# Down-projections of the prompt as seven block products, and small VectorE operations with one SBUF operand

## The chip, the core and the metric

The kernel runs on one core of a Trainium2 chip. Its engines work side by side, each through its own queue: TensorE (PE) multiplies matrices into the eight banks of PSUM, VectorE (DVE), ScalarE (ACT) and GpSimd (POOL) work on rows, and SyncE (SP) issues the transfers. The metric is the device time of one execution in microseconds. The time of a kernel is the median of its runs.

## What is computed

The reference is a two-layer streaming encoder for 1024 prompt tokens and 8 x 16 sample tokens, 1152 rows of 1024 features in float32. Layer 0 has windowed attention with sinks, layer 1 chunk-band attention on keys and values that are projected once from the output of layer 0. In each layer the attention is followed by a gated MLP with a causal convolution. Both parts end in a layer norm over the residual:

```python
u = h @ w_up                      # 1024 -> 2 x 2816
y = conv_b                        # width 3, along the tokens
for tap in range(CONV_W):
    y = y + conv_w[tap] * ue[:, tap:tap + T]
a, g = jnp.split(y, 2, axis=-1)
out = (jax.nn.gelu(g) * a) @ w_down   # 2816 -> 1024: the down-projection
...
x = layer_norm(DEEPNORM_ALPHA * x + (1 + g_f) * f, ln_g[l, 1], ln_b[l, 1])
```

## The kernel before

**Operands in two parts.** Every matmul operand is kept as a rounded part (hi) and the rest (lo), and a product is three matmuls: lo x hi, hi x lo and hi x hi. `split` (L176) makes them: a cast on ScalarE (L167) writes hi, and a subtraction (L178) with two SBUF inputs writes lo, on VectorE or on GpSimd as the caller says.

**Order.** The program is written out in order, and a scheduler places the instructions of each engine from that order, from the buffers that are free, and from a model of the time. `Ring` (L55) hands out buffers in turn, so a buffer that is still in use makes the next writer wait. SyncE issues all the transfers through one queue.

**Up-projection** (`ffn`, L1218). The 2816 hidden features are 22 blocks of 128. Blocks 0 and 1 are made by plain products (`plain`). The other 20 (`spair`) make one value block and one gate block together by seven block products instead of eight (`products`, L1131; the matmul is L1203): the token rows of H are split in halves of 64 tokens within each tile, the weights in halves of their inputs, and sums of blocks stand on both sides. For each row block GpSimd makes four weight sums of 128x512 (L1151 to L1154), ScalarE and VectorE split seven half weights into the ring `sub` of eight half slots, and the PSUM results are added up by VectorE (L1164) or copied by ScalarE (L1162, L1171). Then follow the convolution (L1289 on ScalarE, L1250 on VectorE, L1259 on GpSimd for the sample rows), the gelu (L1296), the product with the value half on GpSimd (L1297), and the store of the gated block of 1152 tokens to `actD` in DRAM (L1298). In layer 0 the modulation vectors of later parts (`ada`) are multiplied in the background of this stage.

**Down-projection** (`down`, L1350). The nine token tiles (8 prompt tiles, and the sample tile 8) are taken in three groups of three. For each group all 22 weight blocks are loaded again (128x1024, 512 KB) with their activations (128x384, 192 KB). `fetch` splits the weights through ScalarE and GpSimd, the activations through ScalarE and VectorE (L1379). `mm` (L1386) runs three matmuls of 512 columns for each tile and each output half. At the end of a group `evict` multiplies the six banks by the gate (L1399, VectorE), and `tail` reads the residual (L1405 in layer 0, L1411 and L1414 in layer 1) and norms the row. In the last group the last 4 or 6 weight blocks (`KEEP`) are kept back and done tile by tile, so that a tile can be finished while the next one is multiplied.

**Tails.** In layer 0 `norm_tail` (L1002) takes the statistics (`stats`, L971 with L975 to L979, and `rsqrt`, L962), norms the row on VectorE (L1006), transposes it on PE (L1016), applies the next modulation by L1028 (ScalarE) or L1024 (VectorE, the chunks in `VA`) and `sample_affine` (L1050, L1051), copies the transposed row (L1032), splits it into H (GpSimd), scales it (L1039, L1040), and stores three rows of 512 KB. In layer 1 `norm_last` (L983) ends the row either by two VectorE operations (L993, L994; tiles in `VT`) or by ScalarE, GpSimd and VectorE in turn (L997, L998, L999).

**After layer 0** `kv` (L824) projects V for nine tiles in two halves, and K by seven products. Its block sums on the token side (`tsums`, L1100) need the normed rows of all tiles.

**Small operations.** In the attention of layer 0 the sink is added to the row sums (L613 for four elements, L699 for one), and `rsqrt` ends with a product of two single columns (L969). All of these have two SBUF inputs.

## Time and profile before

| | us |
|---|---|
| median of 3 runs | 2810.72 (2810.69 to 2818.3) |
| the profiled execution | 2808.31 |
| its span, first to last instruction | 2806.5 |
| down stage of layer 0 / layer 1, from the start of its first to the start of its last matmul | 285.2 / 276.0 |

In the rows of the profile, `PE` is TensorE, `PEld` its weight loads, `DVE` VectorE, `ACT` ScalarE, `POOL` GpSimd and `SP` SyncE. A group of instructions is written as line, engine, operation, output<-inputs by tile name, form and count, then busy us, the mean ns of one, and the idle time of its engine in front of it with what ended that. Where a row has three numbers with slashes, they are the shortest, the median and the longest duration in ns. The names are those of the program: F and ws hold float32 data, wh, wl and X weights, H the input rows, xa (X1) the sums of rows or the activations, C small vectors.

### The profile page before, as it was taken

How to read it: one execution, taken by the hardware profiler on the slowest of the kernel's cores; microseconds unless marked ns; L12 is line 12 of the kernel's file. 1: busy time of each engine (PE TensorE's matmuls, PEld its weight loads, DVE VectorE, ACT ScalarE, POOL GpSimd, SP SyncE). 2: the span in 40 equal slices, each digit the busy share in tenths (PEclk: the TensorE clock that was granted, in tenths of full speed). 3: DMA queues.
4: the chain of work that ended last, by engine and by line, in shares of the span. 5: the costliest groups of instructions: out<-in, count | busy, mean ns of one | idle time of the engine just before them, and what ended most of it. 6: DMA issues, size and time to landing. Idle time of an engine off the chain costs nothing.

```text
span 2806.5 us, 46569 instructions
## 1 busy us (share of the span) xinstructions
PE 2701.0 (96%) x17398; PEld 2384.3 (85%) x17398; DVE 1898.8 (68%) x3622; ACT 1307.8 (47%) x2607; POOL 1117.7 (40%) x755
## 2 busy tenths in 40 slices
PE   7999889999999999999999999989999999999997
PEld 5897768989999998777898888867899999998886
DVE  4376768776666684766854667766887777774764
ACT  3375633533333343443536666663444444444442
POOL 2132523444333457565220121242444333458662
PEclk9999999999999999999999999999999999999999
DMA  7656434474444446665757457763432222247662
GB/s 291 212 157 198 146 98 173 146 250 142 143 156 145 142 132 220 214 225 195 266 199 268 120 153 192 221 202 122 170 123 71 72 80 71 71 143 256 210 199 76
DMA packets 205187, 467.96 MB, mean 167 GB/s; under 512 B 34752, under 2 KB 97936, under 8 KB 204960
## 3 DMA queue, kind: packets, MB, share of 16 engines
q1 hardware_dynamic: 204960, 464.98, 51.0%
q8 instruction: 137, 2.24, 0.3%
q14 instruction: 90, 0.74, 0.1%
HBM read 365.17 MB, written 109.17 MB: 169 GB/s over the span
## 4 chain that ended last, share of the span: by engine, by line
PE 40%; DVE 4%; DMA 3%; ACT 2%; issue 1%; POOL 0%; SPq 0%; POOLq 0%; DVEq 0%; ACTq 0%
PE PS L1203 18%; PE PS L1386 10%; PE PS L296 4%; PE PS L309 4%; PE PS L590 1%; PE PS L568 1%; PE PS L540 1%; DVE F L507 1%; DMA F<-hmD 1%; PE PS L543 1%; ACT F L919 1%; PE PS L717 0%; DVE wl L178 0%; DMA F<-hD 0%; DVE xa L178 0%
## 5 line engine op out<-in xcount | busy, mean ns | idle before, releaser
L1203 PE MATMUL PS<-H,wh 128*128 128x320 f32 (+1 forms) x2752 | 427.9, 298 | 0.0
L1203 PEld LDWEIGHTS PS<-H,wh 128*128 128x128 f32 x2752 | 390.3, 192 | 0.4 <-issue 0.4
L1164 DVE TENSOR_TENSOR F<-PS,F 128x256 f32<-128x256 f32 (+1 forms) x446 | 197.7, 453 | 199.7 <-PE PS L1203 198.9
L167 ACT CAST wh<-F 128x512 fp32r<-128x512 f32 (+3 forms) x265 | 168.0, 645 | 328.3 <-PE PS L1203 186.6
L1379 DVE TENSOR_TENSOR xa<-xa 128x384 fp32r<-128x384 f32 x132 | 180.8, 1379 | 190.5 <-ACT xa L167 189.0
L1250 DVE SCALAR_TENSOR_TENSOR F<-F 128x1024 f32<-128x1024 f32 x320 | 258.9, 855 | 4.5 <-ACT F L1289 3.4
L178 DVE TENSOR_TENSOR wl<-F,wh 128x512 fp32r<-128x512 f32 (+2 forms) x236 | 215.0, 924 | 61.9 <-ACT wh L167 61.5
L1203 PE MATMUL PS<-H,wl 128*128 128x320 f32 (+1 forms) x1376 | 244.0, 300 | 8.7 <-ACT F L1171 7.2
L296 PE MATMUL PS<-H,wh 128*128 128x384 f32 (+1 forms) x1152 | 225.1, 339 | 0.0
L1386 PE MATMUL PS<-wh,xa 128*128 128x512 f32 x696 | 222.0, 395 | 0.0
L178 POOL TENSOR_TENSOR wl<-ws,wh 128x1024 fp32r<-128x1024 f32 x59 | 148.6, 2523 | 178.8 <-ACT wh L167 144.1
L1203 PEld LDWEIGHTS PS<-H,wl 128*128 128x128 f32 x1376 | 205.1, 192 | 16.9 <-ACT F L1171 7.7
L1203 PE MATMUL PS<-xa,wh 128*128 128x320 f32 (+1 forms) x1408 | 216.6, 296 | 1.4 <-DVE xa L178 1.4
L167 ACT CAST wh<-ws 128x512 fp32r<-128x512 f32 (+1 forms) x159 | 126.8, 804 | 190.8 <-PE PS L1203 94.8
L296 PEld LDWEIGHTS PS<-H,wh 128*128 128x128 f32 x1152 | 200.9, 189 | 1.3 <-issue 0.8
L1203 PEld LDWEIGHTS PS<-xa,wh 128*128 128x128 f32 x1408 | 197.4, 189 | 2.1 <-DVE xa L178 1.7
L1259 POOL TENSOR_TENSOR F<-F 128x16 f32<-128x16 f32 x88 | 47.8, 543 | 312.4 <-DVE F L1250 220.5
L1386 PEld LDWEIGHTS PS<-wh,xa 128*128 128x128 f32 x696 | 130.6, 188 | 30.7
L167 ACT CAST xa<-xa 128x384 fp32r<-128x384 f32 x132 | 67.4, 513 | 187.6 <-DMA xa<-actD 181.9
L309 PE MATMUL PS<-wh,H 128*128 128x512 f32 (+1 forms) x576 | 145.7, 367 | 1.4 <-DVE F L1095 0.8
L628 POOL TENSOR_TENSOR F<-F,X 64x512 f32<-64x512 f32 x62 | 79.5, 1282 | 169.6 <-DVE F L604 147.7
L1297 POOL TENSOR_TENSOR F<-F 128x1152 f32<-128x1152 f32 x44 | 119.8, 2722 | 49.5 <-DVE F L1250 31.3
(269 smaller groups left out, 6193.0 us busy)
## 6 DMA issues: line engine op xcount, KB each, us to landing
ws<-in_wdn_dram SPq DMA_DIRECT2D x66, 512.0 KB
F<-in_wdn_dram SPq DMA_DIRECT2D x66, 512.0 KB
ws<-in_adaw_dram SPq DMA_DIRECT2D x64, 512.0 KB
actD<-F SPq DMA_DIRECT2D x44, 576.0 KB
xa<-actD SPq DMA_DIRECT2D x132, 192.0 KB
ws<-in_wup_dram SPq DMA_DIRECT2D x49, 512.0 KB
F<-in_adaw_dram SPq DMA_DIRECT2D x48, 512.0 KB
F<-in_wup_dram SPq DMA_DIRECT2D x39, 512.0 KB
```

Of the source, the lines that this page charges most:

```text
L167: nc.scalar.copy(out, in_)
L178: self.eng(el).tensor_sub(lo, src, hi.bitcast(F32))
L296: mm = self.nc.tensor.matmul(out[:, 0:n], w[a][:, k * 128 : k * 128 + 128], H[:, p, k, s0 : s0 + n], start=i == 0, stop=i == 23)
L309: self.nc.tensor.matmul(out[:, 0:n], H[:, p, j * kn + k, t0 : t0 + 128], w[a][:, k * n : k * n + n], start=i == 0, stop=i == 23,)
L628: self.eng("v" if last else "p").tensor_mul(on[r, q], on[r, q], rb[r, :])
L1164: nc.vector.tensor_add(d, v(ps), a if len(a.shape) == 3 else v(a))
L1203: self.pairmm = nc.tensor.matmul(ps[:, 0:m], w[a][:, k * 128 : k * 128 + 128], x(p, k, n), start=start and c == 0, stop=c == 11, skip_grou ...
L1250: nc.vector.scalar_tensor_tensor(o, u, cw[:, cc, i : i + 1], o, op0=ALU.mult, op1=ALU.add)
L1259: nc.gpsimd.tensor_add(y3[:, :, 0:2], y3[:, :, 0:2], E4[:, cc])
L1297: nc.gpsimd.tensor_mul(yg, yg, ya)
L1379: nc.vector.tensor_sub(lo, raw, hi.bitcast(F32))
L1386: self.downmm = nc.tensor.matmul(ps, a[p][:, i * 128 : i * 128 + 128], w[q][:, hf * 512 : hf * 512 + 512], start=j == 0 and c == 0, stop=j ...
```

## The change

**Seven products for the down-projection.** Two neighbouring weight blocks (an even one and an odd one) form a pair; there are 11 pairs. The prompt is split in two halves of four tiles, the output in two halves of 512 columns. Per pair, GpSimd makes four sums of the activations (`act_sums`) and four of the weights (`weight_sums`), during the up-projection, and both go to DRAM (`actS`, `wT`). Then come seven products one after the other, in the order 1, 2, 5, 6, 3, 7, 4, each over the 11 pairs with four tiles: one weight half and one activation half per step. The sample tile is no part of the seven: it rides as a fifth tile in products 1, 2, 5 and 6, with plain operands. The results are combined on ScalarE and VectorE between the products. Both splits of a step now have their subtraction on VectorE.

**What moves with it.** The gated rows get three fixed buffers (one for the value half, two for the gate half) in place of a ring of three, because the sums overwrite two of them in place. One of the four weight slots becomes the buffer of the weight sums, so `sub` has six half slots. The tails of tiles 8, 0, 1, 2 and 3 run inside products 3 and 7, those of 4 to 7 behind product 4. In layer 0 these last four alternate with the first five V tiles of `kv`. The norm of the tails of layer 0 goes from VectorE to ScalarE (`norm_rows`), all modulations to ScalarE (`VA` is empty), and the scaling product to GpSimd. The tiles X2 and the first weight slot are taken anew with another type between the stages.

**Small operations.** L969, L699 and L996 become operations with one SBUF input and a scalar column; L613 becomes a reduction over a pair of columns.

The core of the diff:

```diff
-GR = ((0, 1, 2), (6, 7, 8), (3, 4, 5))
-GB = ((6, 7, 0, 1, 2, 3), (4, 5, 6, 7, 0, 1), (2, 3, 4, 5, 6, 7))
-TBG = ((2, 3), (0, 1), (0, 1))
+NK = NFF // 2
 NPL = 2
 KEEP = (4, 6)
+TAILS = ({1: 8}, {0: 0, 2: 1, 5: 2, 8: 3}, {})
...
-        NW = 4
+        NW = 3
         wh = mem.tile([128, NW, 1024], F32R, name="wh")
         wl = mem.tile([128, NW, 1024], F32R, name="wl")
         ws = mem.tile([128, 2, 1024], F32, name="ws")
-        self.wslots = [(wh[:, i], wl[:, i]) for i in range(NW)]
+        self.wslots = [None] + [(wh[:, i], wl[:, i]) for i in range(NW)]
         self.w2 = (wh, wl)
+        self.take_w0(F32R)
...
-            nc.vector.tensor_add(L[:, cs], L[:, cs], M[:, cs])
+            nc.vector.tensor_reduce(out=L[:, cs], in_=LM[:, cs, :], op=ALU.add, axis=mybir.AxisListType.X)
...
-                nc.vector.tensor_add(rs, rs, e)
+                nc.vector.tensor_scalar_add(rs, rs, e)
...
-        nc.vector.tensor_mul(r, r, t)
+        nc.vector.tensor_scalar_mul(r, r, t)
...
-            nc.vector.tensor_mul(m, s, r)
+            nc.vector.tensor_scalar_mul(m, s, r)
...
+    def norm_rows(self, x):
+        mean, r = self.stats(x)
+        m = self.sm.next()[:, 0:1]
+        self.nc.vector.tensor_scalar(m, mean, r, -1.0, op0=ALU.mult, op1=ALU.mult)
+        self.nc.scalar.activation(x, x, AF.Identity, bias=m, scale=r)
...
+            if j % 2:
+                nc.sync.dma_start(self.actD[j], yg)
+                self.pend.append(j // 2)
+            else:
+                for r in (slice(0, 512), slice(1024, 1152)):
+                    nc.sync.dma_start(self.actD[j][:, r], yg[:, r])
+
+        def act_sums():
+            for m in self.pend:
+                a11, a21 = ygate[0][:, 0:512], ygate[0][:, 512:1024]
+                a12, a22 = ygate[1][:, 0:512], ygate[1][:, 512:1024]
+                nc.gpsimd.tensor_add(a22, a21, a22)
+                nc.gpsimd.tensor_sub(a21, a11, a21)
+                nc.gpsimd.tensor_sub(a11, a22, a11)
+                nc.gpsimd.tensor_sub(a12, a12, a11)
+                for i in range(2):
+                    nc.sync.dma_start(self.actS[m, i], ygate[i][:, 0:1024])
+            self.pend = []
+
+        def weight_sums(m):
+            b11, b12, b21, b22 = (t[:, o : o + 512] for t in self.w0 for o in (0, 512))
+            for i in range(2):
+                nc.sync.dma_start(self.w0[i], I["wdn"][l, 2 * m + i])
+            nc.gpsimd.tensor_sub(b11, b12, b11)
+            nc.gpsimd.tensor_sub(b12, b22, b12)
+            nc.gpsimd.tensor_sub(b22, b22, b11)
+            nc.gpsimd.tensor_sub(b21, b22, b21)
+            for i in range(2):
+                nc.sync.dma_start(self.wT[l][m, i], self.w0[i])
...
+                if i == 1:
+                    act_sums()
+                if i == 2 and j in wsum:
+                    weight_sums(wsum.index(j))
...
+        def weight(src, ring=None):
+            hi, lo = subs.next()
+            raw = ring.next() if ring else lo.bitcast(F32)
+            nc.sync.dma_start(raw, src)
+            self.split(raw, hi, lo, "a", "v")
+            return hi, lo
+
+        def act(src, sample=None):
+            n = 512 if sample is None else 640
+            hi, lo = (t[:, 0:n] for t in acts.next())
             raw = lo.bitcast(F32)
+            nc.sync.dma_start(raw[:, 0:512], src)
+            if sample is not None:
+                nc.sync.dma_start(raw[:, 512:640], sample)
+            self.split(raw, hi, lo, "a", "v")
+            return hi, lo
+
+        def mm(ps, a, i, w, first, last):
+            for c, (p, q) in enumerate(((1, 0), (0, 1), (0, 0))):
+                self.downmm = nc.tensor.matmul(
+                    ps,
+                    a[p][:, i * 128 : i * 128 + 128],
+                    w[q],
+                    start=first and c == 0,
+                    stop=last and c == 2,
+                    skip_group_check=True,
+                ).ins
+
...
+        def fetch(q, m):
+            e, o = 2 * m, 2 * m + 1
+            w2 = None
+            if q == 1:
+                a, w = act(prompt(e, lo_half), sample(e)), weight(wdn[e][:, lo_half], early)
+            elif q == 2:
+                a, w = act(prompt(o, lo_half), sample(o)), weight(wdn[o][:, lo_half], early)
+            elif q == 5:
+                a, w = act(actS[m, 1][:, hi_half], sample(e)), weight(wT[m, 0][:, lo_half])
+                w2 = weight(wdn[e][:, hi_half], late)
+            elif q == 6:
+                a, w = act(actS[m, 0][:, lo_half], sample(o)), weight(wT[m, 1][:, hi_half])
+                w2 = weight(wdn[o][:, hi_half], late)
+            elif q == 3:
+                a, w = act(actS[m, 1][:, lo_half]), weight(wdn[o][:, hi_half], late)
+            elif q == 7:
+                a, w = act(actS[m, 0][:, hi_half]), weight(wT[m, 0][:, hi_half])
+            else:
+                a, w = act(prompt(o, hi_half)), weight(wT[m, 1][:, lo_half])
+            return a, w, w2 or w
+
+        def product(q, banks, bs=None, new=True, keep=0, hook=None):
+            for m in range(NK - keep):
+                a, w, w2 = fetch(q, m)
+                for i in range(4):
+                    mm(self.bank(banks[i]), a, i, w, new and m == 0, m == NK - 1)
+                if bs is not None:
+                    mm(self.bank(bs), a, 4, w2, q in (1, 5) and m == 0, q in (2, 6) and m == NK - 1)
+                if hook:
+                    hook(m)
...
+        A, B = (0, 1, 2, 3), (5, 6, 7, 0)
+
+        def start(m):
+            if m == 2:
+                act_sums()
+            if m == 6:
+                with self.tc.issue_after(self.downmm):
+                    self.ln_gates(l, 1)
+                    self.ln_rows(l, 1)
+
+        rings = None
+        product(1, A, 4, hook=start)
+        aff = affs()
+        for i in range(4):
+            nc.scalar.copy(p1[i], self.bank(A[i]))
+        product(2, A, 4, new=False)
+        for i in range(4):
+            gate(c11[i], self.bank(A[i]), i, 0)
+        gate(cs[0], self.bank(4), 8, 0)
+        product(5, B, 4)
+        for i in range(4):
+            nc.scalar.copy(q5[i], self.bank(B[i]))
+        product(6, B, 4, new=False)
+        for i in range(4):
+            nc.vector.tensor_add(u4[i], self.bank(B[i]), p1[i])
+        gate(cs[1], self.bank(4), 8, 1)
+
+        def tails(k):
+            def hook(m):
+                if m in TAILS[k]:
+                    t = TAILS[k][m]
+                    tail(t)
+                    rows(*{0: (3,), 1: (4, 5), 2: (6,), 3: (7,)}.get(t, ()))
+
+            return hook
+
+        subs = Ring(subs.items + more)
+        rings = Ring([zt]), Ring([self.hf])
+        rows(8, 0)
+        product(3, B, new=False, hook=tails(0))
+        for i in range(4):
+            nc.vector.tensor_add(p1[i], self.bank(B[i]), p1[i])
+        C, E = (1, 2, 3, 4), (7, 0, 1, 2)
+        rings = Ring([zt, self.w0[0]]), hfr
+        rows(1, 2)
+        product(7, C, hook=tails(1))
+        rings = Ring([zt]), hfr
+        for i in range(4):
+            nc.vector.tensor_add(u4[i], self.bank(C[i]), u4[i])
+            nc.vector.tensor_sub(q5[i], u4[i], q5[i])
+            gate(u4[i], u4[i], 4 + i, 1)
+        keep = KEEP[l]
+        subs = Ring(subs.items[0 : NK - len(more)] + more if l == 0 else subs.items)
+        product(4, E, keep=keep, hook=tails(2))
+        kept = [(m, fetch(4, m)) for m in range(NK - keep, NK)]
+        for i in range(4):
+            for m, (a, w, _) in kept:
+                mm(self.bank(E[i]), a, i, w, False, m == NK - 1)
+            nc.vector.tensor_sub(q5[i], q5[i], self.bank(E[i]))
+            gate(q5[i], q5[i], 4 + i, 0)
+            if l:
+                tail(4 + i)
+            else:
+                head(4 + i)
+        if not l:
+            self.take_w0(F32R)
+            ev = [X2[:, o : o + 1024].bitcast(F32R) for o in (1024, 3072)], [X2[:, 4096:4608]]
+            self.kvrun = self.kv(*ev)
+            next(self.kvrun)
+            for i in range(4):
+                next(self.kvrun)
+                tail(4 + i)
```

238 lines of the change are left out of this document (123 added, 115 removed).

## Prediction

> **What bounds the kernel now.** I read the head of the page, then the busy times by stretch, then single lines.
>
> ```profile
> span 2806.5 us, 46569 instructions
> PE 2701.0 (96%) x17398; PEld 2384.3 (85%) x17398; DVE 1898.8 (68%) x3622; ACT 1307.8 (47%) x2607; POOL 1117.7 (40%) x755
> ```
>
> TensorE (PE) is busy in all but 105.5 of 2806.5 us: a matmul taken away in a full stage is time gained, as long as the feeders keep up.
>
> ```profile
> 2525.00:2755.00 230.00, 230.00 (x991) 185.84 (x990) 138.66 (x145) 103.33 (x142) 159.73 (x63) 1.00 0.65 214
> 2133.40:2357.20 223.80, 223.80 (x1682) 223.80 (x1682) 172.81 (x251) 95.04 (x160) 89.65 (x70) 1.00 0.23 75
> 641.30:844.00 202.70, 202.70 (x1596) 186.35 (x1595) 133.63 (x207) 76.66 (x128) 81.87 (x64) 1.00 0.43 148
> ```
>
> Columns: window, its length, then busy us and count of PE, weight loads, VectorE (DVE), ScalarE (ACT), GpSimd (POOL), granted clock, DMA share, GB/s. First row: down-projection of layer 1. The other two: ten row blocks of up-projection in layer 1 (22.4 us each) and eight in layer 0 (25.3 us each). PE is full in all three, at clock 1.00.
>
> **Part 1, the matmuls.** A down matmul comes every 230.00/991 = 0.232 us. Before, a layer has 22 weight blocks x 9 token tiles x 2 halves x 3 terms = 1188. After, the prompt needs 7 products x 11 pairs x 4 tiles x 3 = 924, and the sample tile 4 x 11 x 3 = 132: 1056. So 264 fewer in two layers, all of the same shape on a full engine: 264 x 0.232 = **-61.3 us**. [...]
>
> **Part 2, the block sums in the up-projection.** GpSimd gets 10 x 4 activation sums and 11 x 4 weight sums per layer (four more come in the down stage), all 128x512 with two SBUF inputs. The nearest rows are the same operation, and the VectorE operations of that stage:
>
> ```profile
> L1151 POOL TENSOR_TENSOR F<-F x5: 1292/1292/1293, 2148.5 to 2327.5; 128x512 f32<-128x512 f32 x5
> L1297 POOL TENSOR_TENSOR F<-F x10: 2687/2692/2698, 2140.2 to 2341.6; 128x1152 f32<-128x1152 f32 x10
> L178 DVE TENSOR_TENSOR wl<-F,wh x50: 680/693/3030, 2137.9 to 2355.0; 128x512 fp32r<-128x512 f32 x50
> L178 DVE TENSOR_TENSOR wl<-F,wh 128x512 fp32r<-128x512 f32 x50 | 48.5, 970 | 12.0 <-ACT wh L167 12.0
> L178 DVE TENSOR_TENSOR wl<-ws,wh 128x512 fp32r<-128x512 f32 x20 | 27.4, 1372 | 2.6 <-ACT wh L167 2.6
> L167 ACT CAST wh<-F 128x512 fp32r<-128x512 f32 (+3 forms) x265 | 168.0, 645 | 328.3 <-PE PS L1203 186.6
> L1164 DVE TENSOR_TENSOR F<-PS,F x100: 410/453/495, 2134.1 to 2356.0; 128x256 f32<-128x256 f32 x50, 128x320 f32<-128x320 f32 x50
> DVE F L1164 <- PE PS L1203: 36.4, 50, 0.9
> ```
>
> The split of the same shape takes 0.693 us or up to 3.03, about one L1297 (2.69) more: a VectorE operation with two SBUF inputs stands still while GpSimd computes. L1164, whose second input lies in PSUM, never passes 0.495. The 70 splits took 48.5 + 27.4 = 75.9 us where 70 x 0.693 = 48.5 would do: 27.4 us held, 31% of GpSimd's 89.65.
>
> The sums add 84 x 1.292 = 108.5 us to GpSimd per layer, 5.4 per row block over 20 blocks. At 31% VectorE loses 1.7 per block, at 100% 5.4. Its idle time per block is (223.80 - 172.81)/10 = 5.1 us in layer 1 and (202.70 - 133.63)/8 = 8.6 in layer 0. So averaged it fits, and VectorE waits for PE at present (36.4 us), not PE for it. But all eight sums of a pair are issued in the even block: 8 x 1.292 = 10.3 us against 5.1. What evens it out is the lead of the splits: the casts (L167) wait for PE to free a slot (186.6 us), so the whole ring is filled ahead of PE. The ring shrinks from eight half slots to six. Behind a held split stand the PSUM additions (L1164), and a bank that is not emptied stops PE. A second new wait is on ScalarE: the sums overwrite the gated rows in place and are stored, and only then may L1289 write the next ones, with casts and PSUM copies queued behind it.
>
> ```profile
> 2162.89 2.69 POOL L1297 TENSOR_TENSOR F<-F 128x1152 f32<-128x1152 f32 x1 [1.82 <-DVE F L1164]
> 2167.34 1.29 POOL L1153 TENSOR_TENSOR F<-ws 128x512 f32<-128x512 f32 x1 [1.76 <-DVE wl L178]
> 2175.76 1.35 ACT L1289 ACTIVATE F<-F 128x1152 f32<-128x1152 f32 x1
> ```
>
> From the end of L1297 (2165.6) to that L1289 there are 10.2 us, for the store of the row, four sums (5.2) and two stores: tight. On SyncE the four transfers of the weight sums and two of the activation sums per pair stand in a stage whose DMA share is 0.23 to 0.43. Ends: 0, and the whole excess of every even block with nothing made good, (10.3 - 5.1) x 10 + (10.3 - 8.6) x 10 = 69 us. The average is what the rows carry, so I stay near the low end: **+8 us** in both layers.
>
> **Part 3, feeding the shorter steps.** A step is now 12 matmuls (2.8 us) or 15 (3.5). All splits go to VectorE; GpSimd's weight splits leave the stage.
>
> ```profile
> L1379 DVE TENSOR_TENSOR xa<-xa 128x384 fp32r<-128x384 f32 x56 | 80.6, 1450 | 85.2 <-ACT xa L167 85.1
> L1399 DVE TENSOR_TENSOR F<-PS,F 128x512 f32<-128x512 f32 x12 | 8.0, 682 | 1.9 <-PE PS L1386 1.9
> L1379 DVE TENSOR_TENSOR xa<-xa x132: 531/1258/3035, 1035.8 to 2769.2; 128x384 fp32r<-128x384 f32 x132
> L167 ACT CAST xa<-xa 128x384 fp32r<-128x384 f32 x60 | 30.9, 515 | 85.1 <-DMA xa<-actD 84.3 <-DVE xa L1379 0.9
> L167 ACT CAST wh<-ws 128x1024 fp32r<-128x1024 f32 x17 | 17.7, 1048 | 10.0 <-PE PS L1386 7.0 <-DMA ws<-in_wv_dram 3.0
> L1028 ACT ACTIVATE F<-PS,C 128x128 f32<-128x128 f32 x20 | 7.5, 456 | 7.4 <-POOL H L178 7.4
> L1040 DVE TENSOR_TENSOR F<-F 128x1024 f32<-128x1024 f32 x6 | 10.1, 1681 | 0.0
> L1050 DVE TENSOR_TENSOR F<-PS,C 128x128 f32<-128x128 f32 x24 | 5.3, 281 | 4.7 <-POOL H L178 4.7
> L975 DVE BATCH_NORM_STATS2 C<-F 128x6 f32<-128x512 f32 x12 | 7.7, 678 | 0.0
> L1414 DVE CUSTOM_DVE_ANT_0 F<-F,C x6: 737/752/2597, 2609.2 to 2709.1; 128x512 f32<-128x512 f32 x6
> GB/s 284 139 182 234 368 221 247 247 200 182 138 199 184 208 246 201 184 348 60 242 393 227 282 256 210 140 200 223 241 178 232 361 197 255 280 217 151 104 149 75
> ```
>
> The activation split ran at 1.45 us where 0.53 is its free time: with GpSimd gone it falls. Products 1, 2, 5 and 6 are safe: the heaviest step has a split of 640 columns (0.84 by the slope from 384 to 512) and two of 512, 2.2 us of 3.5; the casts, 0.73 + 2 x 0.62 (both between 515 ns and 1048 ns), 2.0.
>
> The last three (3, 7, 4) are not. PE: 33 steps x 12 x 0.232 = 92 us. VectorE: splits 33 x 2 x 0.69 = 45.5; combining the blocks 12 x 0.68 out of PSUM and 12 x 0.69 in SBUF, 16.4; five tails in layer 0 of some 5.9 each (gate 0.69, two additions of 0.69, statistics 2 x 0.68, small ones some 1.2, L967 the longest of them with 0.27, L1040 some 1.28 free) = 30, and 16 small ones more for the sample tile (as L1050), about 4. Before the last matmul that is 91 us, and GpSimd's ten tail operations of 2.4 us hold it for 31% to 100% of 24 us: 98 to 115 against 92. In layer 1 a tail has two L1414 in place of the additions, no statistics, and at its end L999 or two operations of 1.28: some 5.2 us. There 45.5 + 16.4 + 9 x 5.2 = 109, with GpSimd's five to seven operations 113 to 125, stand against 92 and the 15 behind the last matmul. In front of this seven activation buffers let splits run ahead by up to 7 x 1.38 = 10 us. ScalarE has 33 x 1.24 + 5 x 7.4 (eight L1028 make 3.7 of it) = 78, enough. The DMA peak is product 7 of layer 0: 11 x 0.52 MB of loads and 16 x 0.52 MB for four tails, 14.2 MB in 31 us; the fastest slice shown, 393 GB/s, needs 36. Ends: 0, and 2 x (115 - 92) = 46 with nothing run ahead. I take **+14**, below the middle, for the lead of 10 in each layer.
>
> **Part 4, ends and seams.**
>
> ```profile
> 1325.00:1450.00 125.00, 121.74 (x712) 109.90 (x711) 90.52 (x194) 56.17 (x128) 32.56 (x23) 0.99 0.64 228
> 2797.96 1.24 ACT L997 ACTIVATE F<-F,C 128x1024 f32<-128x1024 f32 x1 [1.18 <-DVE C L996]
> 2799.28 2.34 POOL L998 TENSOR_TENSOR F<-F 128x1024 f32<-128x1024 f32 x1 [6.93 <-ACT F L997]
> 2801.65 1.23 DVE L999 TENSOR_TENSOR F<-F 128x1024 f32<-128x1024 f32 x1 [3.79 <-POOL F L998]
> 2802.91 0.33 SPq L1000 DMA_DIRECT2D out_y_dram<-F  x1
> 2791.60:2806.50 14.90, 0.16 (x1) 0.00 (x0) 5.74 (x15) 2.68 (x4) 3.09 (x2) 0.66 0.17 70
> ```
>
> V tiles between the last tails of layer 0 can gain at most the 3.3 us that PE idles there; four tails instead of three behind the last block cost up to 10. The last tile, now 7, ends with two VectorE operations (2 x 1.28) for 4.9 us of three engines, but four tiles come 18 x 0.232 = 4.2 us apart at 5 to 6 us of VectorE, so the 14.9 us behind the last matmul stay. SyncE issues 220 loads per down stage instead of 132, one in 1.1 us at 0.33 each: hidden. I take **0**, from -5 to +10.
>
> **Part 5, the small operations.**
>
> ```profile
> L969 DVE TENSOR_TENSOR C<-C x36: 104/160/2374, 415.2 to 2797.5; 128x1 f32<-128x1 f32 x36
> L699 DVE TENSOR_TENSOR C<-C x16: 128/159/3328, 189.4 to 385.0; 128x1 f32<-128x1 f32 x16
> L613 DVE TENSOR_TENSOR F<-F x32: 140/164/2321, 115.1 to 371.7; 128x4 f32<-128x4 f32 x32
> L969 DVE TENSOR_TENSOR C<-C 128x1 f32<-128x1 f32 x36 | 25.5, 711 | 0.8
> L699 DVE TENSOR_TENSOR C<-C 128x1 f32<-128x1 f32 x16 | 9.1, 570 | 2.0 <-ACT C L698 2.0
> L613 DVE TENSOR_TENSOR F<-F 128x4 f32<-128x4 f32 x32 | 12.2, 381 | 5.0 <-ACT F L612 4.7
> L967 DVE TENSOR_SCALAR C<-C x36: 258/272/276, 414.7 to 2797.0; 128x1 f32<-128x1 f32 x36
> ```
>
> Operations on one to four elements take 0.16 us in the median and up to 2.3 or 3.3; L967, the form that L969 and L699 become, never passes 0.276. L613 becomes a reduction, whose second input is gone too; no row shows it, and I take it like L967. Means less medians: 36 x 0.55 + 16 x 0.41 + 32 x 0.22 = 33 us of VectorE at most, nearly all beside a PE that is busy: **-2**, ends 0 and -33. [...]
>
> **Sum.** -61.3 + 8 + 14 + 0 - 2 = -41.3. The profiled execution took 2808.3 us; 2767.0. The median shown lies 2.4 above it (2810.7): **2769**.
>
> **Rivals.** (a) Everything is hidden: -61.3 - 2, 2747. For it: PE full, VectorE averages below its period. Against: even blocks overfull, last products too. (b) VectorE becomes the bound of products 3, 7 and 4: 46 in place of 14, 2801. For it: 115 against 92. Against: the lead and GpSimd's light load there. (c) Slower: the sums in the even blocks hold VectorE and ScalarE past the PSUM deadlines and the odd blocks don't repay. 69 in place of 8: 2830. Place: each even block of the up-projection; it decides from about 2.5 us lost per pair of blocks (49 us over 20 pairs eat what parts 1, 3 and 5 leave). Against: splits lead PE by a whole ring.
>
> **How the numbers follow.** Forecast 0.54 (own range 2752 to 2790), (a) 0.10, (b) 0.18, (c) 0.18. 0.3% is 8.4 us, about what a measurement of this kernel can tell from no change: under 2802 lie the forecast, (a) and 0.08 of (b), 0.72; within, 0.10 of (b); slower (c), 0.18. The range leaves out most of (c) only: 2744 to 2824.
>
> **What would show it.** Down stages of about 245 us each with matmuls still 0.232 apart; idle PE in products 3, 7, 4 waiting for VectorE (b); up blocks still 22.4 and 25.3 us, or even ones longer, with PE waiting for L1164, L1171 or L1289's successors (c); L969 under 0.3 us. Fewer than 264 matmuls gone, or a lower granted clock in the down stages, would break part 1.

## The result and the profile after

The changed kernel takes **2845.41 us** (median of 6 runs, 2837.46 to 2850.4) against 2810.94 (6 runs, 2808.1 to 2818.3): ratio 1.0115, 95% interval 1.0096 to 1.0135. It is slower by 1.15%; the forecast was 2769, faster. The time lies outside the range of 2744 to 2824, on the side of rival (c).

The profiled execution of the changed kernel took 2844.65 us. The head of its page and the busy times:

```profile
span 2842.6 us, 47206 instructions
PE 2676.1 (94%) x17134; PEld 2356.5 (83%) x17134; DVE 2027.0 (71%) x3850; ACT 1348.0 (47%) x2752; POOL 1106.9 (39%) x808
```

TensorE is busy for 24.9 us less than before (2701.0) and is idle for 166.5 us, before 105.5. The 264 matmuls that went are worth 61.3 us; most of the difference goes with the clock, whose mean granted value fell from 0.987 to 0.975 (an estimate: 1.2% of 2701 us are 33). VectorE is busy for 128 us more. Where that happens shows when the span is divided at the starts of the first and last matmuls of the stages (L1203 and L1386 before, L1229 and L1466 after):

| stage | before, us | after, us | difference |
|---|---|---|---|
| start to the first block product | 541.9 | 537.6 | -4.3 |
| up-projection, layer 0 | 508.8 | 527.1 | +18.3 |
| down-projection, layer 0 | 285.2 | 265.0 | -20.2 |
| to the key projections | 51.9 | 58.8 | +6.9 |
| key and value projections | 96.5 | 106.6 | +10.1 |
| attention of layer 1, output projection, plain blocks | 575.0 | 580.2 | +5.2 |
| up-projection, layer 1 | 456.1 | 489.7 | +33.6 |
| down-projection, layer 1 | 275.9 | 257.2 | -18.7 |
| behind the last matmul | 15.2 | 20.4 | +5.2 |

Each column is one execution. Where two runs below share the code of an up-projection, its length agrees within 3.3 us (the change, e5 and e9; e10b and e11); the first stretch differs by up to 3.8 us between such runs, and the attention stretch by 2.8, so the -4.3 and the +5.2 there say little.

The down-projections did get shorter, by 38.9 us. The up-projections, whose matmuls the change leaves alone, lost 51.9. Here are stretches of the changed kernel (columns as in the prediction); the first two are up-projection of layer 1, the next two of layer 0, the last is down-projection of layer 1.

```profile
2108.00:2158.00 50.00, 42.61 (x298) 41.76 (x297) 49.29 (x47) 17.93 (x31) 46.48 (x29) 0.93 0.54 193
2258.00:2308.00 50.00, 50.00 (x377) 49.99 (x376) 43.75 (x57) 20.00 (x35) 29.21 (x20) 1.00 0.26 93
...
588.00:638.00 50.00, 42.49 (x328) 38.83 (x327) 34.35 (x43) 17.76 (x27) 36.47 (x25) 0.90 0.89 321
...
800.00:900.00 100.00, 100.00 (x790) 91.83 (x789) 70.29 (x104) 38.53 (x64) 54.02 (x37) 1.00 0.49 165
...
2570.00:2800.00 230.00, 224.27 (x944) 178.72 (x943) 143.14 (x243) 119.16 (x195) 18.39 (x9) 0.99 0.70 227
```

The up-projections are not slow throughout. In the first row VectorE is busy for 49.29 of 50 us and GpSimd for 46.48, and TensorE issues 298 matmuls (in the two stretches of 50 us behind it VectorE is busy for 42.26 and 45.11 us); in the second row GpSimd has 29.21 and TensorE its full 377. Between them, at about 2247 us, the last weight sums are done: they depend on nothing but their own buffer, so the eleven groups were issued back to back at the front of the stage, one per 17 us, within the first eight of the 22 blocks, and not one per pair of blocks (45 us).

What TensorE waits for in that stage is in the view of waits (us in total, times, longest us), which was empty for the kernel before from 2100 to 2500 us:

```profile
PE PS L1229 <- DVE F L1190: 20.1, 10, 5.6
```

These are the PSUM additions that the prediction named (L1164 before, L1190 now). The additions themselves are not slow: from 2110 to 2250 us L1190 takes 481 and 416 ns in the mean (320 and 256 columns), L1164 before 487 and 422. What stands in front of them is, as the groups of instructions from 2110 to 2250 us show (busy us, mean ns), first before, then after:

```profile
L1250 DVE SCALAR_TENSOR_TENSOR F<-F 128x1024 f32<-128x1024 f32 x27 | 34.5, 1278 | 0.0
...
L1250 DVE SCALAR_TENSOR_TENSOR F<-F 128x120 f32<-128x120 f32 x14 | 4.7, 339 | 0.0
```

```profile
L1277 DVE SCALAR_TENSOR_TENSOR F<-F 128x1024 f32<-128x1024 f32 x21 | 38.4, 1830 | 0.9 <-ACT F L1316 0.8
...
L1277 DVE SCALAR_TENSOR_TENSOR F<-F 128x120 f32<-128x120 f32 x10 | 13.7, 1370 | 0.0
...
L1349 POOL TENSOR_TENSOR w0f<-w0f 128x512 f32<-128x512 f32 x8 | 14.9, 1865 | 1.0 <-DMA w0f<-in_wdn_dram 0.9
```

The convolution taps (L1250, now L1277) have two SBUF inputs. In the mean the long one goes from 1278 to 1830 ns, the short one from 339 to 1370. One by one it is plainer: in the same stretch 18 of the 20 short taps (128x112 and 128x120) take 1.33 to 1.38 us and the other two 0.32, so a short tap is held by some 1.03 us or not at all. Each of the 18 began while a GpSimd sum was running and ended 0.13 to 0.15 us behind that sum's end: it stood until the sum was over. And GpSimd stood too: its sum (L1349) takes 1865 ns in the mean, where L1151 before took 1292.

The small operations (L699, L613 and L969 before), from the start to 540 us (first two) and from 400 us on (last):

```profile
L711 DVE TENSOR_SCALAR C<-C 128x1 f32<-128x1 f32 x16 | 3.3, 207 | 2.3 <-ACT C L710 2.3
...
L625 DVE TENSOR_REDUCE F<-F 128x4 f32<-128x8 f32 x32 | 5.0, 156 | 6.0 <-ACT F L624 5.4
...
L988 DVE TENSOR_SCALAR C<-C 128x1 f32<-128x1 f32 x36 | 7.4, 212 | 0.9
```

Against 9.1, 12.2 and 25.5 us before, VectorE saves 31 us.

### The profile page after: what moved, and what is told of

It is laid out like the page before. It is cut to its first block, busy times and chain, and to the rows that moved or that the text cites. A ratio compares the mean times of both kernels' runs of the same rounds, so it can differ in the third digit from the quotient of the medians.

```text
span 2842.6 us, 47206 instructions
## 1 busy us (share of the span) xinstructions
PE 2676.1 (94%) x17134; PEld 2356.5 (83%) x17134; DVE 2027.0 (71%) x3850; ACT 1348.0 (47%) x2752; POOL 1106.9 (39%) x808
## 5 line engine op out<-in xcount | busy, mean ns | idle before, releaser
L1229 PE MATMUL PS<-H,wh 128*128 128x256 f32 (+1 forms) x2624 | 409.7, 299 | 0.0
L1466 PE MATMUL PS<-wh,xa 128*128 128x512 f32 x1144 | 366.9, 399 | 11.9 <-DVE F L1584 5.3
L1229 PEld LDWEIGHTS PS<-H,wh 128*128 128x128 f32 x2624 | 374.4, 193 | 0.0
L1277 DVE SCALAR_TENSOR_TENSOR F<-F 128x1024 f32<-128x1024 f32 x320 | 312.9, 1025 | 28.1 <-ACT F L1316 27.8
L177 ACT CAST wh<-F 128x512 fp32r<-128x512 f32 (+2 forms) x234 | 137.1, 594 | 316.5 <-PE PS L1229 203.7
L1190 DVE TENSOR_TENSOR F<-PS,F 128x320 f32<-128x320 f32 (+1 forms) x446 | 196.6, 451 | 123.5 <-PE PS L1229 121.6
L1466 PEld LDWEIGHTS PS<-wh,xa 128*128 128x128 f32 x1144 | 215.4, 189 | 69.5 <-ACT H L177 6.1
L1229 PE MATMUL PS<-H,wl 128*128 128x256 f32 (+1 forms) x1312 | 235.4, 301 | 24.4 <-ACT F L1197 15.3
L1466 PE MATMUL PS<-wl,xa 128*128 128x512 f32 x572 | 227.0, 397 | 0.2
L1229 PEld LDWEIGHTS PS<-H,wl 128*128 128x128 f32 x1312 | 196.6, 193 | 34.3 <-ACT F L1197 16.3
L1229 PE MATMUL PS<-xa,wh 128*128 128x320 f32 (+1 forms) x1328 | 207.5, 299 | 0.0
L188 DVE TENSOR_TENSOR xa<-xa 128x640 fp32r<-128x640 f32 (+1 forms) x154 | 122.5, 801 | 112.8 <-ACT xa L177 112.3
L1229 PEld LDWEIGHTS PS<-xa,wh 128*128 128x128 f32 x1328 | 189.8, 192 | 0.0
L177 ACT CAST xa<-xa 128x640 fp32r<-128x640 f32 (+1 forms) x154 | 104.0, 682 | 162.8 <-DMA xa<-actD 110.8
L188 DVE TENSOR_TENSOR wl<-ws,wh 128x512 fp32r<-128x512 f32 (+1 forms) x149 | 166.2, 1120 | 10.3 <-ACT wh L177 10.2
L1324 POOL TENSOR_TENSOR F<-F 128x1152 f32<-128x1152 f32 x44 | 123.7, 2810 | 52.1 <-DVE F L1277 40.8
L1229 PE MATMUL PS<-xa,wl 128*128 128x320 f32 (+1 forms) x664 | 122.9, 307 | 21.2 <-DVE F L1190 20.7
```

The source lines that it names most:

```text
L177: nc.scalar.copy(out, in_)
L188: self.eng(el).tensor_sub(lo, src, hi.bitcast(F32))
L1190: nc.vector.tensor_add(d, v(ps), a if len(a.shape) == 3 else v(a))
L1229: self.pairmm = nc.tensor.matmul(ps[:, 0:m], w[a][:, k * 128 : k * 128 + 128], x(p, k, n), start=start and c == 0, stop=c == 11, skip_grou ...
L1277: nc.vector.scalar_tensor_tensor(o, u, cw[:, cc, i : i + 1], o, op0=ALU.mult, op1=ALU.add)
L1324: nc.gpsimd.tensor_mul(yg, yg, ya)
```

## The experiments

Each was timed in alternation with the kernel before, so ratios compare across them. The last two columns are the up-projections of layers 0 and 1, read from each profile as in the table above.

| run | ratio to before, 95% interval | up 0, us | up 1, us |
|---|---|---|---|
| the change | 1.0115 [1.0096, 1.0135] | 527.1 | 489.7 |
| e1_pinned | 1.0213 [1.0200, 1.0226] | 534.7 | 504.0 |
| e2_no_weight_sums | 1.0008 [0.9996, 1.0020] | 517.5 | 465.1 |
| e3_vector_sums | 1.0076 [1.0061, 1.0092] | 522.3 | 484.3 |
| e4_small_ops | 0.9972 [0.9959, 0.9986] | 508.0 | 457.8 |
| e6_odd_blocks | 1.0106 [1.0085, 1.0126] | 527.2 | 483.1 |
| e7_no_sums | 0.9935 [0.9910, 0.9960] | 516.2 | 455.3 |
| e5_tail_va | 1.0150 [1.0121, 1.0180] | 528.6 | 489.2 |
| e9_tails_early | 1.0113 [1.0089, 1.0136] | 526.3 | 491.1 |
| e10b_vector_odd | 1.0114 [1.0088, 1.0139] | 530.6 | 487.0 |
| e11_vector_odd_tails | 1.0124 [1.0101, 1.0146] | 527.3 | 488.0 |
| e12_one_input | 1.0096 [1.0066, 1.0126] | 533.6 | 470.4 |
| e13_one_transfer | 0.9896 [0.9866, 0.9926] | 508.6 | 455.7 |

**First question: bunching, volume or transfers?** Theory A: it is the crowding of the weight sums at the front. Theory B: their volume, wherever it lies. Theory C: their transfers.

e1_pinned:

```diff
-        E.tensor_sub(a21, a12, S2)
+        self.poolop = E.tensor_sub(a21, a12, S2).ins
...
-            nc.gpsimd.tensor_sub(b11, b12, b11)
+            with self.tc.issue_after(self.poolop):
+                nc.gpsimd.tensor_sub(b11, b12, b11)
...
```

> The changed kernel, with one thing moved: the four weight sums of a pair are issued on GpSimd behind the last of a block's own four sums, so one group per pair, about 45 us apart, instead of all eleven groups at the front of each up-projection. Nothing is left out. Theory A (the bunching costs: eleven groups one per 17 us beside 27 us blocks, then 22.4 us blocks): the up-projections fall from 527 and 490 us to about 510 and 458, the time from 2845 to 2795-2810. Theory B (the volume of the sums costs, wherever they lie, because every GpSimd operation holds VectorE back): the blocks are all 1 us longer, the time stays at 2835-2850. Theory C (the transfers of raw weights and sums cost): they are spread by this too, so it would also fall; the run with the sums left out tells C from A.

It became slower by another 1% instead. **Theory A falls**, though the sums now also stand at another place in the block; the second question takes that up. TensorE now loses a little in every pair of blocks, all through the stage. One stretch of it, and behind it its waits from 2100 to 2500 us:

```profile
2300.00:2400.00 100.00, 93.69 (x688) 92.63 (x687) 86.72 (x103) 38.02 (x66) 67.38 (x45) 0.98 0.37 131
```

```profile
PE PS L1229 <- DVE F L1190: 25.1, 16, 2.4
```

Its timeline shows one of these waits whole (start, length, engine, line), VectorE, GpSimd and TensorE together:

```profile
2317.60 6.18 DVE L1277 SCALAR_TENSOR_TENSOR F<-F 128x1024 f32<-128x1024 f32 x4
2318.79 2.28 POOL L1349 TENSOR_TENSOR w0f<-w0f 128x512 f32<-128x512 f32 x1
...
2321.15 1.29 POOL L1350 TENSOR_TENSOR w0f<-w0f 128x512 f32<-128x512 f32 x1
...
2323.70 0.68 DVE L188 TENSOR_TENSOR wl<-F,wh 128x512 fp32r<-128x512 f32 x1
...
2324.31 0.48 DVE L1190 TENSOR_TENSOR F<-PS,F 128x320 f32<-128x320 f32 x1
...
2324.84 0.97 PE L1229 MATMUL PS<-xa,wl 128*128 128x320 f32 x4 [1.97 <-DVE F L1190]
```

Four taps, two long and two short, are 3.2 us by the rows of before (2 x 1.278 and 2 x 0.33); here they take 6.18, with three GpSimd operations beside them (2.28 and 1.29 us above; the third, L1180 with 1.77 us, had begun before the first tap). The PSUM addition comes behind them in VectorE's order, so the bank is emptied late, and TensorE stands for 1.97 us. At this place, behind the block's own sums, the weight sums meet VectorE's taps.

e2_no_weight_sums:

```diff
-            nc.gpsimd.tensor_sub(b11, b12, b11)
-            nc.gpsimd.tensor_sub(b12, b22, b12)
-            nc.gpsimd.tensor_sub(b22, b22, b11)
-            nc.gpsimd.tensor_sub(b21, b22, b21)
```

> The changed kernel without the four GpSimd operations of the weight sums: raw weights are stored in their place, so five of the seven products take wrong right operands and the output isn't the reference's; loads, stores and the rest are kept, and stay bunched at the front. Theory A and theory B (GpSimd's operations cost): up-projections of about 505 and 456 us, 2790-2805 in all. Theory C (transfers cost): they are as dense as before or denser, so the up-projections stay near 527 and 490 and the time at 2835-2850.

Level with before, so the weight sums are worth 1% by themselves. Of the 33.6 us in layer 1, 24.6 go with them (489.7 to 465.1), although the transfers are a little denser (DMA share 0.62 from 2100 to 2200 us, in the change 0.57). **Theory C falls** for that stage.

e3_vector_sums:

```diff
-                nc.vector.tensor_add(d, v(ps), a if len(a.shape) == 3 else v(a))
+                self.dveop = nc.vector.tensor_add(d, v(ps), a if len(a.shape) == 3 else v(a)).ins
...
-            nc.gpsimd.tensor_sub(b11, b12, b11)
+            with self.tc.issue_after(self.dveop):
+                nc.vector.tensor_sub(b11, b12, b11)
...
```

> The changed kernel with the four weight sums of a pair on VectorE, behind its addition for the second product of the block, one group per pair. Nothing is left out. Theory A: VectorE gets 2.8 us per pair (four times 0.69 us), which its 5 us idle per block cover, and GpSimd has only the activation sums left: up-projections near 510 and 457 us, 2793-2808 in all, level with the pinned GpSimd sums. Theory B (GpSimd's volume): 5-15 us faster than the pinned GpSimd sums. If VectorE is short instead, the blocks grow by 1.4 us: about 2825.

0.4% better than the change, but 19 us of layer 1's stage are still lost (484.3, without weight sums 465.1). The sums were planned as 31 us of VectorE work in that stage (11 x 2.8). They took 53, 4.8 us per pair, because in nine of the eleven groups the first sum met GpSimd's product (L1324, 2.68 us) and waited it out:

```profile
L1349 DVE TENSOR_TENSOR w0f<-w0f x11: 683/2742/2750, 2085.7 to 2508.1; 128x512 f32<-128x512 f32 x11
```

So this run is not free of GpSimd's holds either; what 2.8 us of VectorE's own work would cost is not shown.

e7_no_sums (e2, and):

```diff
-                nc.gpsimd.tensor_add(a22, a21, a22)
-                nc.gpsimd.tensor_sub(a21, a11, a21)
-                nc.gpsimd.tensor_sub(a11, a22, a11)
-                nc.gpsimd.tensor_sub(a12, a12, a11)
```

> The changed kernel without any of the eight GpSimd sums of a pair (weight sums and activation sums): the raw blocks are stored in their place, so the products take wrong operands and the output isn't the reference's; every load and store is kept. If the sums are the whole loss in the up-projections (theories B and D): 508 and 456 us, as before the change, and 2788-2798 in all. If the further transfers or the changed order of the block cost something: they stay at 517 and 465 as without the weight sums alone, 2805-2810.

Layer 1 is back at 455.3 (456.1 before): there the eight sums of a pair are the whole loss. Layer 0 keeps 7.4 us. From 2100 to 2500 us e3 (first row) and e7 have the same VectorE time, and yet e3 issues 5% fewer matmuls:

```profile
2100.00:2500.00 400.00, 387.18 (x2854) 380.88 (x2854) 339.80 (x463) 158.03 (x272) 230.24 (x153) 1.00 0.38 136
2100.00:2500.00 400.00, 400.00 (x3005) 400.00 (x3004) 340.26 (x450) 168.26 (x286) 182.29 (x123) 1.00 0.36 125
```

At TensorE's full pace e3's VectorE would be busy for some 358 of the 400 us (an estimate: 339.80 x 3005/2854). It has idle time left, and that did not hide the sums.

e13_one_transfer (e7, and the same for the other reads of wT):

```diff
-                if i == 2 and j in wsum:
+                if i == 2 and j == 2:
...
-                a, w = act(prompt(o, hi_half)), weight(wT[m, 1][:, lo_half])
+                a, w = act(prompt(o, hi_half)), weight(wT[0, 1][:, lo_half])
```

> The run without any sums, with ten of the eleven pairs of weight transfers of each layer's up-projection (1 MB in, 1 MB out) left out too: the products read the one stored pair in all eleven places, so the output isn't the reference's. Without the sums the up-projections took 516 and 455 us, against 509 and 456 before the change. If the bunched transfers cause the 7 us that are left in layer 0 (DMA share 0.92 and 0.84 in its first 100 us, 0.69 and 0.54 before): 508-511 us there, 455 in layer 1, and 2778-2786 in all. If the first block's changed order or the buffer that the weight slots lost causes it: it stays at 514-518, 2784-2792.

Layer 0 is back as well: 508.6 (508.8 before). The first 100 us of that stage, without sums and then with one pair of weight transfers:

```profile
530.00:580.00 50.00, 42.93 (x318) 39.26 (x318) 32.41 (x56) 18.25 (x34) 14.79 (x12) 0.93 0.92 320
580.00:630.00 50.00, 44.06 (x328) 39.97 (x327) 27.63 (x42) 17.48 (x30) 16.64 (x12) 0.93 0.84 293
```

```profile
530.00:580.00 50.00, 42.71 (x325) 39.23 (x324) 30.38 (x55) 17.70 (x32) 12.34 (x11) 0.93 0.72 235
580.00:630.00 50.00, 48.53 (x381) 44.85 (x381) 35.71 (x50) 19.97 (x34) 20.90 (x15) 1.00 0.62 214
```

In the second 50 us the DMA share falls from 0.84 to 0.62 and TensorE gains 53 matmuls. So theory C holds for a small part, at the front of layer 0, where the weights of the modulation vectors (adaw) are loaded as well. The loss of the up-projections is now accounted for: 45 us for the sums (34 in layer 1, 11 in layer 0), 7 for transfers.

**Second question: does the place in the block count (theory D), or the volume alone (theory B)?**

e6_odd_blocks (the four sums inside the last line; gop is the gating product of `gated`):

```diff
-                if i == 2 and j in wsum:
+                if i == 1 and j in wsum:
...
-        wsum = [2, 3] + list(range(4, NFF - 1, 2))
+        wsum = [2] + list(range(3, NFF, 2))
...
+            with self.tc.issue_after(self.gop):
```

> The changed kernel with the weight sums of a pair moved to the odd block and issued on GpSimd right behind the gating product of the block before, ahead of the block's own sums; the activation sums stay in the even block. Nothing is left out. With all the sums at the front the changed kernel's up-projections took 527 and 490 us, with one group per pair behind the block's own sums 535 and 504. Theory D (what counts is the place in the block: a sum beside VectorE's convolution taps delays the additions behind them, a sum beside the products doesn't): about 515 and 472, 2818-2828 in all. Theory B (the volume: each sum holds VectorE for its own length wherever it lies, and eight more sums per pair use up VectorE's idle time): 530 and 500, 2850-2868, as with one group per pair behind the block's sums.

In between: both. With the same eight sums per pair, the place gives back 21 us of layer 1 (504.0 to 483.1), but 18 stay lost against no weight sums, and as a whole the run is level with the change. VectorE is then at 90% to 92%, and the single waits are short:

```profile
2200.00:2300.00 100.00, 98.27 (x725) 96.65 (x724) 92.10 (x110) 41.68 (x74) 68.11 (x47) 1.00 0.39 132
```

```profile
PE PS L1229 <- DVE F L1190: 7.6, 23, 2.1
```

e10b_vector_odd (e3, and):

```diff
-                if i == 2 and j in wsum:
+                if i == 1 and j in wsum:
...
-        wsum = [2, 3] + list(range(4, NFF - 1, 2))
+        wsum = [3, 4] + list(range(5, NFF, 2))
```

> The changed kernel with the four weight sums of a pair on VectorE, as in the run with VectorE's sums (up-projections 522 and 484 us), but issued from the odd block on (the first in block 3), where no activation sums hold VectorE. Nothing is left out. If the meeting of both kinds of sums in the even block was what cost: up-projection of layer 1 at 468-475 us, 2812-2822 in all. If VectorE's own 2.8 us per pair are simply too much beside GpSimd's holds: 480-486 us and 2825-2832, as before.

487.0 us: the second answer. It is no better than in the even block, in the time as a whole rather worse (1.0114 against 1.0076). Here too GpSimd holds the sums: in layer 1's stage they take 57 us of VectorE, not 31.

e12_one_input (e1, with this in place of the four sums):

```diff
+                for b in (b11, b12, b22, b21):
+                    nc.gpsimd.tensor_scalar_mul(b, b, 1.0)
```

> The changed kernel with the four weight sums of a pair replaced by four GpSimd multiplications by 1.0 of the same 128x512 blocks, at the place of the slow run (one group per pair, behind the block's own sums: up-projections 535 and 504 us). The right operands of five products are then the raw weights, so the output isn't the reference's. It asks which form of a GpSimd operation holds VectorE. If any GpSimd operation on SBUF does, for its own length: four of about 0.6 to 1.3 us, 485-504 us in layer 1, 2828-2865 in all. If only those with two SBUF inputs do: VectorE's taps beside them keep their 1.28 us, 463-468 us, 2803-2812, as with no weight sums at all.

The time as a whole gives the first answer (1.0096 against 1.0008 without any), layer 1 alone lies near the second (470.4). The means of a stretch do not decide, since the block's own sums hold taps in it as well: with neither weight nor activation sums (e7) the short taps of 128x120 still take 854 ns in the mean, here 736.

```profile
L1277 DVE SCALAR_TENSOR_TENSOR F<-F 128x120 f32<-128x120 f32 x12 | 8.8, 736 | 0.0
```

Single operations do. The first two rows are the multiplications and a short tap that began while one was running, the third a short tap that began during a sum:

```profile
L1350 POOL TENSOR_SCALAR w0f<-w0f x40: 1482/1577/2478, 2103.6 to 2492.0; 128x512 f32<-128x512 f32 x40
L1277 DVE SCALAR_TENSOR_TENSOR F<-F x1: 675/675/675, 2210.3 to 2210.3; 128x112 f32<-128x112 f32 x1
L1277 DVE SCALAR_TENSOR_TENSOR F<-F x1: 1374/1374/1374, 2228.1 to 2228.1; 128x120 f32<-128x120 f32 x1
```

From 2100 to 2500 us 22 short taps began during a multiplication: all take 0.68 or 0.69 us and end 0.74 to 0.76 us in front of its end. The 15 that began during a sum of 128x512 take 1.36 to 1.38 and end 0.13 to 0.15 us behind the sum's end. So these one-input multiplications hold the taps too, but by 0.35 us in place of 1.03, although they are no shorter on GpSimd: 1.482 us at least, where the sum takes 1.292. In layer 1 that is worth 34 us (504.0 to 470.4) at the same place, with the same transfers and with GpSimd busier than in e1 (298 against 274 us from 2100 to 2500): what costs there is the hold on VectorE, not GpSimd's time. Why layer 0 loses 16 us by them and layer 1 only 5 stays open.

**Third question: the stretch behind layer 0's down-projection** (58.8 + 106.6 us against 51.9 + 96.5). Two guesses: ScalarE, which took over affine pieces, or the last tails, which now come late.

e5_tail_va:

```diff
-VA = ()
+VA = (4, 5, 6, 7)
```

> The changed kernel with one line back as before: in the tail of a row tile of layer 0, four of the eight affine pieces go to VectorE again and not to ScalarE. Nothing is left out. It is about the 17 us lost between the first layer's down-projection and the end of the key and value projections (58.8 and 106.6 us against 51.9 and 96.5). If ScalarE (39.6 of 58.7 us busy there, 25.5 of 51.9 before) makes the last tails late: 53 and 99 us, 2828-2836 in all. If VectorE or the later start of the tails bounds that stretch: no change or up to 5 us more, 2840-2850.

e9_tails_early:

```diff
-                next(self.kvrun)
                 tail(4 + i)
+                next(self.kvrun)
```

> The changed kernel with the last four row tiles' tails of layer 0 each put ahead of the value projection of a tile, not behind it. Nothing is left out. It is about the rest of the loss behind the first layer's down-projection, where TensorE waits 6.45 us for the block sums of the tokens, whose last tiles leave their tails at 1377-1380 us. If late tails are the cause: the key and value projections fall from 106.6 to about 99 us, the time by 6-10 us to 2832-2838. If that stretch is bound by something else (VectorE's and GpSimd's turns in the tails, the loads behind them): no change, or TensorE waits for the tails' rows instead, 2840-2848.

The first made the stretch longer (64.7 and 106.5): giving the pieces back to VectorE doesn't help. The second took 5.8 us out (55.6 and 104.0), but the time as a whole didn't move beyond its interval. The block sums of the tokens hardly came earlier by it: the first begins at 1379.5 us, in the change at 1380.1. Here are, for the changed kernel, TensorE's wait for them from 1330 to 1500 us and the first of the sums on VectorE; behind them the kernel before:

```profile
PE PS L1229 <- ACT xa L177: 8.2, 2, 6.4
```

```profile
L1135 DVE TENSOR_TENSOR F<-F x9: 409/418/1478, 1380.1 to 1408.1; 128x256 f32<-128x256 f32 x9
```

```profile
L1109 DVE TENSOR_TENSOR F<-F x9: 410/415/425, 1368.7 to 1396.0; 128x256 f32<-128x256 f32 x9
```

They begin 11.4 us later, and 17.5 us later when counted from the last matmul of the down-projection (at 1329.8, before at 1335.9). Two of the buffers that their splits write lie in X2, which now holds rows of two late tiles; that this is the reason was not tried.

e11_vector_odd_tails (e10b and e9 together):

> VectorE's weight sums in the odd block and the last four tails of layer 0 ahead of the value projections, both together. Nothing is left out. The tails alone took 5.8 us out of their stretch (55.6 and 104.0 us against 58.8 and 106.6) and nothing that could be told in the time as a whole. If the two add: 5 us below the odd block's run of this call; if the time is given back later: level with it. Faster than the kernel before (2811) only if the odd block's run reaches 2815.

Level with e10b: what the tails give back (3.8 us in that stretch against e10b) doesn't show in the whole.

**Fourth question: the small operations alone**, on the kernel before.

e4_small_ops:

```diff
-                nc.vector.tensor_add(rs, rs, e)
+                nc.vector.tensor_scalar_add(rs, rs, e)
...
-                nc.vector.tensor_add(L[:, cs], L[:, cs], M[:, cs])
+                nc.vector.tensor_reduce(out=L[:, cs], in_=LM[:, cs, :], op=ALU.add, axis=mybir.AxisListType.X)
```

> The kernel before with the small VectorE operations of softmaxes and norms alone changed (one SBUF operand, the other as a scalar per row; the row sums and exponentials of the first attention side by side and added by a reduction). Nothing is left out. Theory of the prediction: 2 us faster, 2808-2811, which can hardly be told from none. Other theory: the 4.3 us that the changed kernel's start stage lost are theirs, so 2805-2807. If they cost at all, 2812 or more.

Faster by 0.28% [0.14, 0.41], 8 us. This is the only complete version that beats both kernels: the small operations kept, the block products of the down-projections left out.

## Why the prediction was wrong, point by point

- **Part 1, right.** The steps nearly kept their pace (a matmul per 0.238 us of TensorE's busy time from 2570 to 2800 us, 224.27/944, before 0.232) and the matmuls went away: with 61.3 us of matmuls gone, the down-projections lost 38.9. The rest is in Part 3.
- **Part 2, the step that failed:** "The average is what the rows carry, so I stay near the low end". The term was +8 and measured +51.9: sums 45, transfers 7. That lies between the stated ends (0 and 69), and the chain was right: GpSimd's sums held VectorE (a short tap by 1.03 us), additions stood behind the held operations, TensorE stopped (10 times from 2100 to 2500 us, 20.1 us). That a VectorE operation with two SBUF inputs stands still while GpSimd computes was seen beside the two-input sums; beside the one-input multiplications of e12, of 1.48 us or more, a short tap was held for 0.35 us only. That the convolution taps are held beside the splits it did not say. Wrong was the choice between the ends. The argument set VectorE's average idle time (5.1 us per block) against GpSimd's added time (5.4) and called it a fit. In these runs idle time in the average was not free to be used: e3 has some left by the estimate above and loses 19 us. VectorE idles while it waits for TensorE's next product (36.4 us in ten blocks before), and it is late when four taps are due together; e1's timeline shows that at one place (6.18 us in place of 3.2), and that it is the whole reason is not shown. The transfers were put at nothing by the DMA share of 0.23 to 0.43, which leaves out the front of layer 0: its first 100 us had 0.69 and 0.54 before the change. That the sums come in the even block was wrong too: the weight sums came at the front, within the first eight blocks. By e1 the planned place would have been worse.
- **Part 2's second wait**, ScalarE writing the gated rows, is small: in the change TensorE waits 8.9 us for ScalarE's copies (L1197) in layer 0, of which 6.9 are one wait at 548 us that e7 has without any sums too (5.7). With e1's order it waits for them once per pair from 790 us on; whether the gated rows are the reason there is not shown.
- **Part 3, undersized:** +14 became +22 (61.3 less 38.9). (Its VectorE terms for layer 0 add up to 96 us; the 91 leave out 5 without saying which.) Rival (b), VectorE as the bound of the last products, happened in a small part at most: in layer 1's last 97 us TensorE is busy for 93.97 and VectorE for 77.28; in layer 0's last 92 us VectorE is busy for 82.67, and TensorE waits once, 4.0 us, inside product 4 (first row). The other long waits are where one product follows another, as in layer 1 (second and third row):

```profile
PE PS L1466 <- DVE H L188: 4.0, 1, 4.0
...
PE PS L1466 <- DVE F L1584: 3.0, 1, 3.0
PE PS L1466 <- DVE xa L188: 1.8, 1, 1.8
```

- **Part 4, wrong:** 0, from -5 to +10, became +22 (6.9 + 10.1 + 5.2). The tails were counted, the token sums behind them not. Why those sums are late stays open. Behind the last matmul VectorE is busy for 16.57 of 20.4 us with four tiles, where it was 5.74 of 14.9; the prediction had kept the 14.9:

```profile
2822.20:2842.60 20.40, 0.37 (x2) 0.00 (x0) 16.57 (x32) 5.04 (x8) 5.41 (x2) 0.62 0.25 103
```

- **Part 5, right in kind, small in size:** -2 against -8 by e4. L988 is under 0.3 us as forecast (0.216 at most, so this form was not held once in 36), VectorE's 33 us came out as 31; a quarter of it lies on the path, not a sixteenth.
- **The rivals.** (c) named the mechanism, the wait and the deciding loss: the change loses 2.6 us per pair (51.9 over 20), just above its 2.5. The sums alone lose 2.3, so (c) did not decide it by itself: without the transfers, and with Parts 3 and 4 as forecast, the change would have come out about level (-61.3 + 45 + 14 - 2 = -4). It also placed the loss in the even blocks, and the weight sums stood at the front. The reason against it, the lead of the splits, was no help: the late instruction was an addition, which can't lead.

The sum with the measured terms: -61.3 + 52 + 22 + 22 + 1 (start -4.3 and the stretch of attention +5.2) = +36, and the spans differ by 36.1, as they must, since the terms are taken from the same two spans.

## What to carry to other kernels

The sums were not hidden by VectorE's average idle time: 5.4 us of GpSimd per block stood against 5.1 us of it in layer 1, and 34 us were lost. So see at which points of the cycle the idle time lies, and what in-order work stands behind. Where a profile shows one GpSimd operation holding one VectorE operation, price every further one of that form at its full length, in both directions (here a sum held a short tap for 1.03 us, and took 1865 ns itself in place of 1292), and stay near the upper end of the bound when the added time equals the slack. An operation that depends on nothing but its own buffer can be issued long before its place in the source, as the weight sums were, so look up where it went; and run the small edits of a bundle alone, since here they were the gain.

## What the runs showed of the hardware

In the change and in e1 short waits of TensorE went with a lower granted clock, in e3 they did not. In the change's stretch from 2108 to 2158 us TensorE is busy for 42.61 us with 298 matmuls; at the pace of the full stretch (377 in 50.00) those take 39.5. The other 3.1 us go with the clock, 0.93 there (39.5/42.61 is 0.93), and no wait of TensorE between 2100 and 2500 us is longer than 5.6 us. In e1, whose longest wait there is 2.4 us, the clock is 0.97 to 0.98 all through it; in e3, with 23 waits of at most 1.4 us there, it is 1.00.

A short tap, which has two SBUF inputs, that began during a two-input GpSimd sum of 128x512 ended 0.13 to 0.15 us behind the sum, 18 of 18 from 2110 to 2250 us in the change; beside a one-input multiplication of 128x512 it was held for 0.35 us and ended 0.74 to 0.76 us in front of the multiplication's end, 22 of 22 from 2100 to 2500 us in e12. And operations with a single element per row took 0.57 (L699) and 0.71 us (L969) in the mean with two SBUF inputs, up to 3.33 and 2.37, and 0.21 us with one (L711 and L988 in the change), at most 0.216.
